# r's first six column tiles as three Strassen units, product by product, in a hybrid encoder block

## The chip, the cores and the metric

The kernel runs on one core of a Trainium2 chip. The metric is the device time of one execution in microseconds (us). A core has a matrix engine (PE, its weight loads shown as PEld), a vector engine (DVE), an activation engine (ACT), a general engine (POOL) and SyncE (SP), which here issues nearly all DMAs. Each engine takes its instructions in order, and instructions wait for each other by semaphores.

## The reference

One layer with 1024 tokens of width 1024, all in float32. What matters here:

```
h = rmsnorm(x)
q, k, v, r, lr_f, lr_b, u, g_a, g_b = split(h @ w_in)          # r has 1024 columns
o = gla(q, k, v, decay(lr_f)) + flip(gla(flip(q, k, v), decay(lr_b)))   # 4 heads, chunked, both directions
o = per_head_rmsnorm(o) * gla_norm * silu(r)
y_a = o @ w_branch_gla
y_b = pooling(u) @ w_pool_group * pool_scale
x = x + (sigmoid(g_a) * y_a + sigmoid(g_b) * y_b) @ w_out
x = x + swiglu(rmsnorm(x))                                       # w_ffn_in, w_ffn_out
out = rmsnorm(x)
```

## The kernel before

**Precision.** A float32 product is made of three fast ones: each operand is split into a high part (a cast on ACT) and a low part (the source minus the high part, on POOL or DVE, `split_to`, L200), and `products` (L271) multiplies high by high, high by low and low by high into one PSUM bank. `mm3` (L276) does that for one block of 128 x 128 weights and 512 tokens, and then calls `pump` with the work done; the text calls it a triple.

**Side work.** `pump` (L162) is the only clock: it counts triples, and after each hands out what is due. There are four lists. `put_off` (filled by `soon`) holds steps with a delay; `pending` holds splits of weights; `aside` holds generators of jobs (`beside`, L686: load, sum, cast, store, one job each time, every so many triples); `side` holds the attention of a head (`attention`, L816), a generator that yields the number of triples until its next step. So the order of instructions is fixed by counts in the program, not by time. `finish_side` and `finish_beside` run the rest of a list at once.

**Tiles.** Most data lie in 39 slots of 128 x 1024 float32 (`slot`); a load into a slot waits until the slot's last reader is done, and SP waits with it. Weights go through `wts`: four buffers `raw`, six each of `wh` and `wl`. PSUM has eight banks: three for the main products (`ps_mm`), five for the attention and other uses (`ps_g`).

**The order of the work.** The normalised features are split and stay on chip as `hT`: 16 slots, for four pairs of feature blocks, two halves of the tokens, high and low part. Then come the values and q, k of the four heads (`project_qk`, L801); beside them run the attention of the heads, the sums of the feature blocks for later (`feature_sums`, into `f_out`) and the sums of the branch weights (`branch_jobs`, into `s_out`, every 4.2 triples).

After the last k come **r's first six column tiles** (L1257 to L1291): for each tile and each half of the tokens, `feature_major` (L297) adds up eight triples in a bank. During that the attention of head 3 runs in `side`; its steps give up the ACT and DVE between them: logarithms (L843), decays (`decay`, L848, a scan on DVE), exponentials (L877 to L879), the backward sweep of states (`advance`, L910), the scores (L930), and the forward sweep (L1022), which takes the score matrix p, the stored states and the running state `sf`. The first two tiles are copied out and gated later; the others are taken through silu straight away, and `gated` (L1220) multiplies them with the head's output, stored before by heads 0 to 2 in `o_out` and loaded by `load_o`. From the fourth tile on, `feature_parts` loads the feature sums, 512 KB each, and casts and subtracts them into high and low parts for the next stage.

The **next stage** ("gates") computes r's last two tiles, u, and the two gates. It uses Strassen's scheme: two column tiles by two halves of the contraction, times two halves of the contraction by two halves of the tokens, in seven products of four triples (`Unit`, `product`, L1198) instead of eight. The operand sums of the features come from `f_out`; the weight sums are made on DVE as they are needed. Products 1, 2 and 3 use feature blocks of `hT` as they are, the others sums of them:

```
    for p, i, half in ((1, 0, 0), (2, 1, 0), (3, 1, 1)):
        right[p] = [hT.pair(2 * i + c, half) for c in range(2)]
```

Later stages (the branch projection, the output projection, the feed-forward part) use the same scheme.

Of the kernel before, what the change touches and what calls it, by code (L numbers as in the profile page):

```python
# [54 lines left out]
def kernel(  # L55
# [57 lines left out]
    def as_f32(ap):  # L113
        return ap.bitcast(F32)
# [127 lines left out]
    order += [(w_in, KT, R0 + j * P, P) for j in range(KT - 2)]  # L242
# [396 lines left out]

    right = {}  # L640
# [25 lines left out]
    def feature_parts():  # L666
        todo = [(p, c) for p in (6, 5, 7, 4) for c in range(2)]
        wholes = []

        def load_sum():  # L670
            if len(wholes) < len(todo):
                p, c = todo[len(wholes)]
                wholes.append(slot(s="hs"))
                nc.sync.dma_start(wholes[-1][:, :, :], f_out[p][:, c])

        load_sum()
        yield load_sum, None, None
        for n, (p, c) in enumerate(todo):
            yield load_sum, wholes[n][:, :, :], p
# [120 lines left out]

    def project_qk(h, last=False):  # L801
        q = slot(s="q")
        k = slot(s="k")
        for dst, scale in ((q, DK**-0.5), (k, 1.0)):
            final = last and dst is k
            w = take(not final)
            if final:
                value_weights[0].splits(2)
            elif last:
                value_weights.append(ValueWeights())  # L810
            for half in range(2):
                ps = feature_major(w, hT, half)
                nc.scalar.activation(dst[:, half, :], ps[:, :], AF.Copy, scale=scale)
        qk_heads[h] = q, k
# [252 lines left out]
    def load_o(h):  # L1067

        o_heads[h] = [slot(s="ol") for _ in range(2)]
        for half in range(2):  # L1070
            nc.sync.dma_start(o_heads[h][half][:, :, :], o_out[h][half].rearrange("(j p) t -> p j t", p=P))

# [23 lines left out]
    for h in range(HEADS):  # L1096
# [7 lines left out]
        if h == 0:  # L1104
            for ts in ((7,), (6,), (5, 4)):
                pair_products(ts)
            prepare_beside(map(branch_jobs, range(4)), 4.2)
# [110 lines left out]
    raw_r, oT, gated_o = [], {}, []  # L1218

    def gated(j, half, src, sr=None):  # L1220

        sr = t2(s="sr")[:, :] if sr is None else sr
# [4 lines left out]

        src, dst, silu = o_heads[j // 2][half], tiles[half][:, j % 2, :], sr
        if j // 2 < HEADS - 1:
            src = src[:, j % 2, :].rearrange("p (i n b) -> p n i b", i=4, b=SQ)  # L1230
            dst, silu = (t.rearrange("p (n i b) -> p n i b", n=4, b=SQ) for t in (dst, silu))
        else:
            tp = bank(ps_g, "tp")
            for i in range(4):
                nc.tensor.transpose(
                    tp[:, i * P : (i + 1) * P], src[:, i, (j % 2) * P : (j % 2 + 1) * P], ident[:, :]
                )
            src = tp[:, :]
        nc.vector.tensor_tensor(dst, src, silu, op=ALU.mult)
        there.append((j, half))  # L1240
        if len(there) == 4:
            c = j // 2 % 2
            for half, t in enumerate(tiles):
                (gated_o if j < KT - 2 else deferred).append((ob_out[j // 4, half][:, 2 * c : 2 * c + 2, :], t[:, :, :]))
            if j >= KT - 2:
                soon(2, flush)

    def put_by():

        if raw_r:  # L1250
            gated(*raw_r.pop(0))
# [5 lines left out]
    BY, PARTS_FROM = 2, 3  # L1257
    sums_begun = False
    for j in range(KT - 2):
        for h in {1: (0,), 2: (1,), 4: (2,)}.get(j, ()):  # L1260
            load_o(h)
        w = take()
        if j < BY:
            whole_r = slot(s="r")
        if j == 4:
            for _ in range(2):
                gunits[0].load()
        if j == 5:
            gates_ahead.step()
        for n, half in enumerate(reversed(range(2)) if j == KT - 3 else range(2)):  # L1270
            if j >= PARTS_FROM and not sums_begun and (j > PARTS_FROM or not side):
                finish_side()
                finish_beside()
                prepare_beside([feature_parts()], 4, quick=2)
                sums_begun = True
            ps = feature_major(w, hT, half)
            if n == 0:
                flush()
            elif j == 3:
                fetch()  # L1280
                soon(3, store_gated)
            if j < BY:
                nc.scalar.copy(whole_r[:, half, :], ps[:, :])
                raw_r.append((j, half, *[whole_r[:, half, :]] * 2))
            elif (j, half) == (BY, 0):
                soon(4, put_by, partial(gated, j, half, ps[:, :]))
            else:
                put_by()
                gated(j, half, ps[:, :])
            if j == KT - 3 and n == 0:  # L1290
                gates_ahead.step()  # L1291
    for p, i, half in ((1, 0, 0), (2, 1, 0), (3, 1, 1)):
        right[p] = [hT.pair(2 * i + c, half) for c in range(2)]


    sa_out, yb_out = (dram.tile([P, 2, KT, HALF], F32, name=n) for n in ("sa_out", "yb_out"))
# [271 lines left out]
    store_gated()  # L1568
# [613 lines left out]
```

## Time and profile before

| | |
|---|---|
| time, three runs | 1370.26, 1370.83, 1370.83 us; median 1370.83 |
| profiled execution | 1370.65 us; span from the first to the last instruction 1368.9 us |
| clock granted to PE | 0.999 |
| r's six tiles, in the span | about 263.5 to 347.5 us |

In the rows that follow, times are in us from the span's start unless marked otherwise. A row of an engine in order of time has the start, the duration, the engine, the line of the kernel, the operation, what it writes and reads, its shape and a count; in brackets stands the idle time of the engine ahead of it and what ended that. A row of waits has who waited for whom, the total in us, how often, and the longest. Names such as ps (main products), op (the attention's output), sc and p (scores), z (decays), trh and trl (high and low parts of the feature sums) are the program's. PE's matmuls are pipelined, so that the duration of one is more than the interval between two.

### The profile page before, as it was taken

To read this page: it belongs to the slowest core of one execution; us is meant where nothing else is said; L and a number is where in the kernel's file an instruction comes from. 1 tells how busy PE (TensorE), PEld (TensorE's weight loads), DVE (VectorE), ACT (ScalarE), POOL (GpSimd) and SP (SyncE) were. 2 spreads that over 40 slices of the span, in tenths; PEclk is the share of its full clock that TensorE was granted. 3 is DMA by queue.
4 is the path that set the end of the run, shared out by engine and by line. 5 is a ranking of instruction groups with operands and counts; after the bars stand their busy time and mean duration, and the time that the engine had idled before them with its cause. 6 is when DMAs were issued, how large, how long until landed. Compare 5 with 4: busy or idle time off the path is not lost. (4 is left out here: it accounts for less than half of the span.)

```text
span 1368.9 us, 17814 instructions
## 1 busy us (share of the span) xinstructions
PE 1356.6 (99%) x6262; PEld 1128.0 (82%) x6262; DVE 850.3 (62%) x1050; ACT 646.0 (47%) x1175; POOL 755.8 (55%) x561
## 2 busy tenths in 40 slices
PE   9999999999999999999999999999999999999998
PEld 7888888888788888888888888888888888888886
DVE  6975666655545767779873955565565556343375
ACT  7365665765434445554356533333333334444252
POOL 3323723223596547568764386666666667555453
PEclk9999999999999999999999999999999999999999
DMA  7321623327487669996426354555544447975552
GB/s 228 110 95 55 181 81 108 83 64 259 123 274 251 200 186 344 367 372 218 138 76 233 124 174 157 177 177 177 177 156 137 141 141 265 389 294 184 171 214 77
DMA packets 174842, 252.50 MB, mean 184 GB/s; under 512 B 11512, under 2 KB 101152, under 8 KB 174752
## 3 DMA queue, kind: packets, MB, share of 16 engines
q1 hardware_dynamic: 174608, 251.10, 54.5%
q8 instruction: 49, 0.80, 0.3%
q14 instruction: 41, 0.34, 0.1%
q10 hardware_dynamic: 144, 0.26, 0.1%
HBM read 169.27 MB, written 82.05 MB: 184 GB/s over the span
## 5 line engine op out<-in xcount | busy, mean ns | idle before, releaser
L202 POOL TENSOR_TENSOR wl<-fs,wh 128x512 fp32r<-128x512 f32 x124 | 171.8, 1390 | 162.6 <-ACT wh L201 105.1
L274 PE MATMUL ps<-gh,wh 128*128 128x512 f32 x616 | 240.5, 390 | 0.0
L274 PE MATMUL ps<-gl,wh 128*128 128x512 f32 x616 | 239.8, 389 | 0.3 <-DVE gl L1740 0.3
L274 PE MATMUL ps<-gh,wl 128*128 128x512 f32 x616 | 239.7, 389 | 0.0
L202 POOL TENSOR_TENSOR wl<-fraw,wh 128x512 fp32r<-128x512 f32 x93 | 133.0, 1430 | 71.5 <-ACT wh L201 68.9
L202 POOL TENSOR_TENSOR ol<-gor,oh 128x1024 fp32r<-128x1024 f32 (+1 forms) x42 | 101.4, 2417 | 86.0 <-ACT oh L201 71.5
L274 PE MATMUL ps<-hh,wh 128*128 128x512 f32 x356 | 144.5, 406 | 0.7 <-ACT ga L1523 0.7
L274 PE MATMUL ps<-hh,wl 128*128 128x512 f32 x356 | 138.9, 390 | 0.0
L274 PE MATMUL ps<-hl,wh 128*128 128x512 f32 x356 | 138.8, 390 | 0.0
L274 PEld LDWEIGHTS ps<-gl,wh 128*128 128x128 f32 x616 | 115.7, 188 | 24.3 <-DVE gl L1740 0.7
L274 PEld LDWEIGHTS ps<-gh,wl 128*128 128x128 f32 x616 | 115.6, 188 | 24.2
L274 PEld LDWEIGHTS ps<-gh,wh 128*128 128x128 f32 x616 | 115.7, 188 | 24.0 <-DVE sums L1906 0.2
L274 PE MATMUL ps<-oh,oh 128*128 128x512 f32 x308 | 119.8, 389 | 0.0
L274 PE MATMUL ps<-ol,oh 128*128 128x512 f32 x308 | 119.8, 389 | 0.0
L274 PE MATMUL ps<-oh,ol 128*128 128x512 f32 x308 | 119.8, 389 | 0.0
L202 POOL TENSOR_TENSOR wl<-wraw,wh 128x512 fp32r<-128x512 f32 x56 | 94.4, 1714 | 43.4 <-ACT wh L201 43.3
L202 DVE TENSOR_TENSOR ol<-wor,oh 128x1024 fp32r<-128x1024 f32 (+1 forms) x42 | 62.3, 1496 | 68.1 <-ACT oh L201 55.8
L202 POOL TENSOR_TENSOR wl<-raw,wh 128x512 fp32r<-128x512 f32 x34 | 49.7, 1472 | 85.2 <-ACT wh L201 66.2
L201 ACT CAST wh<-fs 128x512 fp32r<-128x512 f32 x124 | 76.0, 615 | 27.1 <-DVE fs L1131 26.1
L274 PEld LDWEIGHTS ps<-hh,wl 128*128 128x128 f32 x356 | 66.8, 188 | 14.2
L274 PEld LDWEIGHTS ps<-hh,wh 128*128 128x128 f32 x356 | 67.0, 188 | 13.3 <-ACT ga L1523 1.1
L274 PEld LDWEIGHTS ps<-hl,wh 128*128 128x128 f32 x356 | 67.0, 188 | 12.3
(282 smaller groups left out, 3077.4 us busy)
## 6 DMA issues: line engine op xcount, KB each, us to landing
fraw<-in_w_ffn_in_dram SPq DMA_DIRECT2D x44, 512.0 KB, 5.9
gor<-g_out SPq DMA_DIRECT2D x35, 512.0 KB, 6.6
fraw<-in_w_in_dram SPq DMA_DIRECT2D x22, 512.0 KB, 6.4
g_out<-s SPq DMA_DIRECT2D x44, 256.0 KB, 2.3
wor<-t_out SPq DMA_DIRECT2D x20, 512.0 KB, 4.7
raw<-in_w_in_dram SPq DMA_DIRECT2D x36, 256.0 KB, 4.2
g_out<-g SPq DMA_DIRECT2D x33, 256.0 KB, 2.6
x<-in_x_dram SPq DMA_DIRECT2D x16, 512.0 KB, 4.6
```

The lines of the kernel that those rows point to most:

```text
L201: nc.scalar.copy(hi, src)
L202: eng.tensor_tensor(lo, src, as_f32(hi), op=ALU.subtract)
L274: nc.tensor.matmul(ps, a[i], b[j], start=first and n == 0, stop=last and n == 2, skip_group_check=onto)
```

## The change

- r's first six column tiles become three Strassen units (`TRIO` = 3) of two tiles. They run **product by product**: product 2 of units 0, 1, 2, then product 5 of all three, and so on in the order 2, 5, 3, 1, 6, 7, 4, with 21 products of four triples in all. Each unit holds one PSUM bank; products 2 and 5 are copied out of it by ACT, 3 goes onto 5's bank and is copied, 1 starts a bank in which 6, 7 and 4 go on, with what the copies hold added by DVE.
- The weight sums for products 3, 5, 6 and 7 of each unit are made beside the attention by POOL (`r_jobs`) and stored to `r_out`; the branch sums go every 2.8 triples instead of 4.2, and `r_jobs` every 2 after them. In the r stage each product loads its 256 KB of weights (`r_load`, five products ahead) and splits them (`r_split`, three ahead); it had been 512 KB and two splits for a whole tile.
- The feature sums are loaded by an explicit list of events in the r stage (`load_sums`, `cast_sum`, `low_sum`): 5's ahead of the stage and at its first products, then 6's, 7's and 4's.
- Each row of r is gated when both its halves are there (`gate_row`); o is loaded by halves (`load_ol`).
- The feature block that product 2 uses is stored to memory after the first head's values (`store_block`) and loaded again near the end of the stage (`load_block_again`), so that its four slots are free between.

The diff, cut to its core:

```
-    order += [(w_in, KT, R0 + j * P, P) for j in range(KT - 2)]
...
+    def r_jobs(u):
+        raw = [slot(F32, (KT, P), "rraw")[:, :, :] for _ in range(2)]
+        a11, a12, a21, a22 = (t[:, 4 * j : 4 * j + 4, :] for t in raw for j in range(2))
+        yield from loading(
+            [w_in[:, c0 : c0 + P].rearrange("(k p) c -> p k c", p=P) for c0 in (R0 + 2 * u * P, R0 + (2 * u + 1) * P)], raw
+        )
+        for op, dst, a, b, p in (
+            (padd, a22, a21, a22, 5), (psub, a21, a11, a21, 7), (psub, a11, a22, a11, 6), (psub, a12, a12, a11, 3)
+        ):
+            yield partial(op, dst, a, b), None, r_out[u][p]
...
-    def feature_parts():
...
+    def load_sums(p):
+        sums_in[p] = [slot(F32R, s="trl")[:, :, :] for _ in range(2)]
+        for c, t in enumerate(sums_in[p]):
+            nc.sync.dma_start(as_f32(t), f_out[p][:, c])
+
+    def cast_sum(p, c):
+        hi, lo = slot(F32R, s="trh")[:, :, :], sums_in[p][c]
+        right.setdefault(p, []).append((hi, lo))
+        nc.scalar.copy(hi, as_f32(lo))
+
+    def low_sum(p, c):
+        hi, lo = right[p][c]
+        nc.vector.tensor_tensor(lo, as_f32(lo), as_f32(hi), op=ALU.subtract)
...
+    R_PRODUCTS = 2, 5, 3, 1, 6, 7, 4
+    r_sequence = [(u, p) for p in R_PRODUCTS for u in range(TRIO)]
...
     def project_qk(h, last=False):
...
+            begun = h == HEADS - 1 and dst is k
+            if begun:
+                finish_beside()
+                load_sums(R_PRODUCTS[1])
+                for n in range(4):
+                    r_load(n)
             for half in range(2):
                 ps = feature_major(w, hT, half)
                 nc.scalar.activation(dst[:, half, :], ps[:, :], AF.Copy, scale=scale)
+                if begun:
+                    r_split(half)
+        if begun:
+            r_load(4)
+            r_split(2)
...
+            store_block()
+            prepare_beside(map(branch_jobs, range(4)), 2.8)
+            prepare_beside(map(r_jobs, range(TRIO)), 2)
...
+    def r_evict(u, p, ps):
+        rows = r_rows[u]
+        if p in (2, 5):
+            rows[p == 5] = slot(s="r")
+        i, half = {2: (0, 0), 1: (0, 0), 3: (0, 1), 6: (0, 1), 5: (1, 1), 7: (1, 1), 4: (1, 0)}[p]
+        dst = rows[i][:, half, :]
+        if p in (2, 5, 3):
+            nc.scalar.copy(dst, ps)
+            return
+        if p != 4:
+            add(dst, ps, dst)
+            ps = dst
+        nc.scalar.activation(dst, ps, AF.Silu)
...
+    for p in R_PRODUCTS:
+        if p not in FIRST[:2] and p != 3:
+            at = TRIO * R_PRODUCTS.index(p)
+            if p != 5:
+                event(at - 5, partial(load_sums, p))
+            event(at - 3, partial(cast_sum, p, 0))
+            event(at - 2, partial(cast_sum, p, 1), partial(low_sum, p, 0))
+            event(at - 1, partial(low_sum, p, 1))
+    for u in range(TRIO):
+        event(11 + u, partial(load_ol, u, 0))
+        event(14 + u, partial(gate_row, u, 0))
+        event(15 + u, partial(load_ol, u, 1))
+        event(19 + u, partial(gate_row, u, 1))
+    event(17, partial(load_block_again, 0))
+    event(18, partial(load_block_again, 1))
+    event(16, *[gunits[0].load] * 2)
+    event(14, finish_side)
...
+    for n, (u, p) in enumerate(r_sequence):
+        if n:
+            flush()
+        r_load(n + 5)
+        r_split(n + 3)
+        for step in r_events.get(n, ()):
+            step()
+        if p in (2, 5, 1):
+            r_banks[u] = bank(ps_mm)
+        ps = r_banks[u]
+        product(lambda p, k: r_weight(u, p, k), p, ps, right)
+        r_evict(u, p, ps[:, :])
```

More of the change, by code (lines that the diff above doesn't have):

```diff
@@ L1226, in gated @@
         tiles, there = oT[j // 2]
[L1228 to L1239, printed above, removed]
+        o = o_heads[j // 2][half]
+        tp = bank(ps_g, "tp")
+        for i in range(4):
+            nc.tensor.transpose(tp[:, i * P : (i + 1) * P], o[:, i, (j % 2) * P : (j % 2 + 1) * P], ident[:, :])
+        nc.vector.tensor_tensor(tiles[half][:, j % 2, :], tp[:, :], sr, op=ALU.mult)
         there.append((j, half))
@@ L1243, in gated @@
             for half, t in enumerate(tiles):
[L1244 to L1251, printed above, removed]
+                deferred.append((ob_out[j // 4, half][:, 2 * c : 2 * c + 2, :], t[:, :, :]))
+            soon(2, flush)
     def store_gated():
@@ L1255, in store_gated @@
             nc.sync.dma_start(*gated_o.pop(0))
[L1257 to L1291, printed above, removed]
@@ L1292, with load_ol, gate_row @@
     for p, i, half in ((1, 0, 0), (2, 1, 0), (3, 1, 1)):
         right[p] = [hT.pair(2 * i + c, half) for c in range(2)]
+    r_rows = [[None, None] for _ in range(TRIO)]
+    r_banks, ol = {}, {}
+    def load_ol(u, i):
+        ol[u, i] = slot(s="ol")
+        nc.sync.dma_start(ol[u, i][:, :, :], o_out[u].rearrange("a (j p) t -> j p a t", p=P)[i])
+    def gate_row(u, i):
+        j, row = 2 * u + i, r_rows[u][i]
+        for half in range(2):
+            dst = row[:, half, :]
+            turned_product(dst, ol[u, i][:, half, :], dst)
+            gated_o.append((ob_out[j // 4, half][:, j % 4, :], dst))
+        soon(3, store_gated)
@@ L1296 @@
+    for step in r_events[len(r_sequence)]:
+        step()
     sa_out, yb_out = (dram.tile([P, 2, KT, HALF], F32, name=n) for n in ("sa_out", "yb_out"))
```

62 lines of the change are left out of this document (42 added, 20 removed).

## The prediction

> **What bounds the kernel now.** I read the totals first, then the waits of the matrix engine, its order of time in the r stage, and last the queues of ACT and DVE there. The totals (busy us, share, instructions):
>
> ```profile
> span 1368.9 us, 17814 instructions
> PE 1356.6 (99%) x6262; PEld 1128.0 (82%) x6262; DVE 850.3 (62%) x1050; ACT 646.0 (47%) x1175; POOL 755.8 (55%) x561
> ```
>
> The matrix engine (PE) is busy all the time, but busy time of pipelined matmuls does not by itself show a limit; its waits do. In the chain of waits, PE rows only (us in total, times, longest):
>
> ```profile
> PE ps L274 <- ACT ga L1523: 1.3, 2, 0.7
> PE ps L274 <- POOL wl L202: 0.6, 2, 0.4
> PE op L274 <- DVE p L202: 0.4, 2, 0.2
> PE op L274 <- ACT p L201: 0.3, 1, 0.3
> ```
>
> The rows make 2.6 us in 1369. So PE's own stream is the bound, and a matmul taken out is worth its issue interval, unless something else then comes late. The interval, from the first and the last of 69 matmuls of the r stage with nothing between them (start us, us):
>
> ```profile
> 263.54 0.39 PE L274 MATMUL ps<-hh,wh 128*128 128x512 f32 x1
> ...
> 278.95 0.40 PE L274 MATMUL ps<-hh,wl 128*128 128x512 f32 x1
> ```
>
> (278.95 - 263.54) / 68 = 0.227 us; three of them, one row block in split precision ("a triple"), 0.68 us. The r stage in three windows (length, then busy us and count of PE, PEld, DVE, ACT, POOL; clock, DMA share, GB/s):
>
> ```profile
> 263.50:300.00 36.50, 36.50 (x186) 30.85 (x186) 22.72 (x38) 26.42 (x52) 14.58 (x14) 1.00 0.41 120
> 300.00:320.50 20.50, 20.50 (x124) 18.26 (x123) 11.73 (x27) 12.24 (x37) 3.55 (x3) 1.00 0.40 129
> 320.50:347.50 27.00, 27.00 (x121) 22.36 (x120) 18.82 (x22) 13.76 (x21) 8.41 (x5) 1.00 0.70 234
> ```
>
> PE never waits in these 84 us. The first two windows also carry the attention of head 3, whose steps run between the triples; there ACT is busy 72% and 60%. That is the cover to watch.
>
> **The change part by part.** *Matmuls.* Six column tiles are 6 x 2 halves x 8 blocks x 3 = 288 matmuls; three units of seven products are 3 x 7 x 4 x 3 = 252. The transposes of head 3's output are as many as before. 36 x 0.227 = **-8.2 us**. [...]
>
> *Weight sums beside the attention.* Twelve POOL operations, six loads of 512 KB, twelve stores of 256 KB, in the steps that the branch sums leave when they go every 2.8 triples and not every 4.2: 31 steps x 4.2 = 130 triples before, 31 x 2.8 + 24 x 2 = 135 after (four times seven steps, three times seven, and three to drain each), and 144 triples lie between their start and the last k projection, where `finish_beside` would run what is left. One operation, and one split:
>
> ```profile
> L715 POOL TENSOR_TENSOR wsum<-wsum x16: 1270/1291/1742, 115.1 to 423.1; 128x512 f32<-128x512 f32 x16
> L202 POOL TENSOR_TENSOR wl<-raw,wh x34: 1271/1294/2549, 34.9 to 329.4; 128x512 fp32r<-128x512 f32 x34
> ```
>
> 12 x 1.29 = 15.5 us more on POOL over some 150 us; behind one of them a split or a q product comes at most 1.3 us late. Bounds: -0.6 (the POOL waits of PE vanish) to +2.6 (two such hits); I take 0. The feature block's four stores and four loads of 512 KB lie on SP; PE used these tiles long before the store and needs the reload only in the next stage.
>
> *The r stage's other work.* Splits go from 12 to 21, evictions on ACT from 16 operations (4 copies, 12 silus) to 21 (9 and 12), DVE gets 9 additions. The eight casts and eight residuals of the feature sums stay eight, but come earlier: before, the first cast was at 321.4, after head 3's attention; now product 5's two stand at the stage's first products, and those of 6 and 7 in the attention's forward sweep. ACT, in order of time, with the idle time ahead in brackets, and the rows of the sums (min/median/max ns):
>
> ```profile
> 264.36 0.64 ACT L813 ACTIVATE k<-ps 128x512 f32<-128x512 f32 x1
> 265.01 1.28 ACT L843 ACT_TABLE_LOAD   x1
> 266.31 2.05 ACT L843 ACTIVATE z<-z 128x512 f32<-128x512 f32 x4
> ...
> 273.74 0.62 ACT L201 CAST wh<-raw 128x512 fp32r<-128x512 f32 x1
> 274.26 0.60 ACT L877 ACTIVATE qe<-z 128x512 f32<-128x512 f32 x1
> ...
> 278.70 0.59 ACT L1283 COPY r<-ps 128x512 f32<-128x512 f32 x1 [2.72 <-PE ps L274]
> ...
> 285.75 0.20 ACT L879 ACTIVATE fac<-tot 128x8 f32<-128x8 f32 x1
> ...
> 297.00 0.59 ACT L201 CAST p<-sc 128x512 fp32r<-128x512 f32 x1
> ...
> 311.40 0.51 ACT L923 ACTIVATE sf<-st,fac 128x256 f32<-128x256 f32 x1 [0.16 <-DVE st L919]
> ...
> 312.61 0.60 ACT L201 CAST wh<-raw 128x512 fp32r<-128x512 f32 x1
> ```
> ```profile
> L709 ACT CAST trh<-hs x8: 1047/1055/1063, 321.4 to 342.4; 128x1024 fp32r<-128x1024 f32 x8
> L700 DVE TENSOR_TENSOR trl<-hs,trh x8: 1212/1218/2322, 324.7 to 347.6; 128x1024 fp32r<-128x1024 f32 x8
> ```
>
> Back to back a 512-column ACT operation takes 0.52 (273.74 to 274.26). DVE's decay, and the scores' residual:
>
> ```profile
> 266.92 0.69 DVE L850 TENSOR_TENSOR la<-la,z 128x512 f32<-128x512 f32 x1 [2.11 <-ACT z L843]
> 267.78 1.23 DVE L862 TENSOR_TENSOR_SCAN z<-la,carry 128x511 f32<-128x511 f32 x1
> 269.24 0.43 DVE L868 TENSOR_TENSOR z<-z,tot 128x256 f32<-128x256 f32 x1
> ...
> 270.43 2.21 DVE L862 TENSOR_TENSOR_SCAN z<-la,carry 128x511 f32<-128x511 f32 x1
> ...
> 297.62 0.69 DVE L202 TENSOR_TENSOR p<-sc,p 128x512 fp32r<-128x512 f32 x1 [0.65 <-ACT p L201]
> ```
>
> First place, product 5 (fourth product, needs its second residual 14 triples into the stage: 263.54 + 14 x 0.68 + 0.23 = 273.3). ACT's queue from 264.36: k's eviction 0.52, three casts 1.56, first sum cast 1.05, table 1.28, logarithms 2.05, an eviction and a cast 1.04, second sum cast 1.05: 272.9. DVE adds 1.22: 274.1. PE waits **0.8**. Bounds: 0 (ACT reaches the first casts earlier) to 1.9 (the residual at its longest, 2.32).
>
> Second place, the score matrix p. The logarithms start at 268.8, not 266.3. From 274.1 DVE does three more decays of 2.75 (266.92 to 269.67) to 3.8 (scan 2.3) and four products or residuals of 0.6: 284.8 to 287.9, with short waits for ACT some 287.2; the fourth exponentials (1.2) end at 288.4, against 285.95 (285.75 + 0.20): 2.4 late. Until p ACT then does three evictions, three casts and a sum cast, 4.2 us, where it had a copy and two casts, 1.6; 0.5 of the rest goes into its idle time. So p's cast moves from 297.0 to 297.0 + 2.4 + 2.1 = 301.5, and p is whole 1.3 later, 302.8. PE's use of it, and of the first forward state sf:
>
> ```profile
> 299.95 0.28 PE L274 MATMUL op<-vh,p 128*128 128x256 f32 x1
> ...
> 303.36 0.59 PE L1035 MATMUL op<-sf,qe 128*128 128x256 f32 x2
> ...
> 311.74 0.27 PE L274 MATMUL op<-vh,p 128*128 128x256 f32 x1
> ...
> 314.00 0.28 PE L274 MATMUL op<-vh,p 128*128 128x256 f32 x1
> ```
>
> 299.95 + 0.8 = 300.75, so PE waits **2.0**. Bounds: 0 (all decays at 2.75, and all bursts in idle time) to 4 (every scan at 2.3 and nothing hidden).
>
> Third place, sf. Between p and the first forward state ACT gets a table load, two silus, two casts and a sum cast (4.4), and DVE two additions and two residuals ahead of it, the second behind that sum cast; sf comes 4.8 after p, PE uses it 3.4 after (303.36 - 299.95): **1.4**, bounds 0 to 2.5. The sweep's later bursts fit: a step is 2.3 us of PE (311.74 to 314.00) and 1.2 of ACT (311.40 to 312.61).
>
> *After the attention* ACT and DVE have room (third window: 51% and 70%). Queued by SP from product 13 up to the block's second half: 1792 + 768 + 1280 + 2048 + 1536 + 1024 KB = 8.65 MB (sums of 4, weights, o, stores of the gated rows, the next unit's weights, the block). The rate that the queues keep up where they are full:
>
> ```profile
> 547.00:582.00 35.00, 35.00 (x155) 28.84 (x154) 25.14 (x25) 18.47 (x31) 21.08 (x14) 1.00 0.98 368
> ```
>
> 8.65 MB / 368 = 23.5 us; PE needs the block's second half 38 triples and two forward steps later, 26 + 2 = 28 us. Cost 0 (bounds 0, and the rival below). The two waits of the next stage (1.3, ACT ga) I leave as they are, bounds -1.3 to +1.3.
>
> Sum: -8.2 + 0.8 + 2.0 + 1.4 = -4.0. The profiled execution took 1370.65 (span 1368.9), 0.2 under the median 1370.83; from the median **1366.8**.
>
> **The rivals.** *All of it is kept.* If ACT's idle time (2.72 in the quoted row alone) takes the added casts, no place costs over 0.3: 1362.6 to 1363. For it: PE waits nowhere in the stage now. Against: the sum of ACT's queue up to product 5 has no idle time left in it.
>
> *The chain eats all of it.* Where POOL works beside it, DVE is slow: the scan at 267.78 took 1.23, most of it before these two splits, and the one at 270.43 took 2.21:
>
> ```profile
> 269.00 2.55 POOL L202 TENSOR_TENSOR wl<-raw,wh 128x512 fp32r<-128x512 f32 x2 [9.24 <-ACT wh L201]
> ```
>
> The residuals took 1.22 at best and 2.32 at worst. If nine more splits hit two scans and four residuals, that is 2 x 1 + 4 x 1.1 = 6.4 more on DVE, of which some 4 reach PE: 1370.8, no change. [...]
>
> *Slower: the reload comes late.* If the queues move what stands from product 13 on at the 234 GB/s of the third window and not at 368, 8.65 MB take 37.0 us, 9 over the 28: 1366.8 + 9 = 1375.8. It turns the gain into a loss from 4.0 us of wait on, that is below 8.65 MB / 32 us = 270 GB/s. For it: weight blocks come in short rows from the input matrix, and SP stands still behind a load that waits for a slot. Against: that window's share is 0.70, so 234 is demand and not the limit.
>
> **How the numbers follow.** The forecast (1364 to 1368.5) gets 0.44, all kept 0.19, eaten 0.25, slower 0.12. 0.2% is 2.7 us, about what a measurement of this kernel tells from no change: faster (under 1368.1) 0.44 + 0.19 less 0.02 that lies above the line, same 0.27, slower 0.12. The range from 1362.6 to 1371.5 leaves out most of the slow case and the edges. The forecast's own range is 1364 to 1368.5.
>
> **What the profile after would show.** Right: 6226 matmuls; in PE's waits, rows of a few tenths to 2 us at ps behind a trl residual near 273, at op behind p near 300, at op behind sf near 305; ACT over 85% busy from 264 to 305. All kept: no such rows and a stage of 75.8 us. Eaten: the same rows, longer, and scans and residuals all over 2 us. Slower: a wait of ps for a DMA at the first product 2 after the r stage. The prediction is wrong if PE waits for wl of the r products, which I cost at nothing (three products, 8 us, ahead), or if slots hold SP back so that these weights come late.

## The result, and the profile after

| | before | after |
|---|---|---|
| median of the runs on one chip | 1370.83 us (4 runs) | 1387.38 us (1386.65 to 1387.83, 4 runs) |
| ratio, 95% interval | | 1.0121 [1.0103, 1.0138] |
| profiled execution; its span | 1370.65; 1368.9 us | 1387.01; 1385.3 us |

The change made the kernel 1.2% slower; the forecast was 0.3% faster. The totals of the page after (span, then busy us, share and number of instructions of each engine):

```profile
span 1385.3 us, 17868 instructions
PE 1355.8 (98%) x6226; PEld 1123.8 (81%) x6226; DVE 855.8 (62%) x1059; ACT 653.0 (47%) x1189; POOL 781.0 (56%) x582
```

The 36 matmuls are gone (6262 to 6226), and yet the span is 16.4 us longer. In the chain of waits, the rows of the matrix engine PE (us in total, times, longest):

```profile
PE ps L273 <- POOL wl L202: 7.5, 4, 6.1
PE op L273 <- ACT p L201: 5.1, 2, 4.9
PE ps L273 <- DVE trl L693: 2.7, 3, 1.3
PE ps L273 <- ACT ga L1603: 1.7, 2, 1.1
PE ps L273 <- ACT wh L201: 1.1, 1, 1.1
PE ps L273 <- DMA hl<-h_out: 1.1, 2, 0.8
```

Before, the four such rows made 2.6 us; now these six make 19.2. PE in order of time shows the two large ones, with the last matmul ahead of each:

```profile
220.76 0.39 PE L273 MATMUL ps<-hl,wh 128*128 128x512 f32 x1
227.21 0.79 PE L273 MATMUL ps<-hh,wl 128*128 128x512 f32 x1 [6.06 <-POOL wl L202]
...
311.04 0.39 PE L273 MATMUL ps<-hh,wl 128*128 128x512 f32 x1
316.32 0.58 PE L273 MATMUL op<-vh,p 128*128 128x256 f32 x1 [4.89 <-ACT p L201]
```

The first lies 42 us ahead of the r stage, in the projection of head 3's q; the second in the r stage, at the score matrix. Behind both the clock is granted by half, as the windows show (busy us and count of PE, PEld, DVE, ACT, POOL; then the clock, DMA share, GB/s):

```profile
224.00:227.00 3.00, 0.00 (x0) 0.00 (x0) 0.76 (x2) 0.45 (x2) 3.00 (x4) 0.50 1.06 315
227.00:230.00 3.00, 2.79 (x8) 2.41 (x9) 0.04 (x1) 0.00 (x0) 3.00 (x5) 0.50 0.56 154
230.00:233.00 3.00, 3.00 (x17) 2.55 (x17) 1.52 (x3) 1.85 (x5) 2.92 (x3) 0.93 0.23 87
...
316.00:318.00 2.00, 1.68 (x6) 1.46 (x7) 1.70 (x3) 0.65 (x2) 0.23 (x1) 0.50 0.36 78
...
320.00:322.00 2.00, 2.00 (x7) 1.71 (x7) 0.69 (x1) 0.97 (x4) 0.17 (x1) 0.50 0.26 58
```

Where the time went, by three places that both traces have: the first of head 3's z matmuls, the first r product, and the first copy of a gate. Before, and after:

```profile
257.16 0.40 PE L825 MATMUL z<-lrT,up 128*128 128x512 f32 x1
262.18 0.39 PE L274 MATMUL ps<-hh,wh 128*128 128x512 f32 x1
352.80 0.58 ACT L1523 COPY ga<-ps 128x512 f32<-128x512 f32 x1
```
```profile
264.57 0.40 PE L887 MATMUL z<-lrT,up 128*128 128x512 f32 x1
269.59 0.39 PE L273 MATMUL ps<-hh,wh 128*128 128x512 f32 x1
369.25 0.58 ACT L1603 COPY ga<-ps 128x512 f32<-128x512 f32 x1
```

The z matmul starts 7.4 us later than before: the wait of 6.06 us and some 1.6 us of work lost to the half clock behind it, less what other places gave. From the first r product to the first copy of a gate it is 99.7 us where it was 90.6; with 8.2 us of matmuls less, that is 17.2 us lost. The waits in this stretch make 10.8 of them, the half clock from 316.3 to 322.6 some 3.1. Of the other 3.3 about 0.16 lie at each of the nine waits, 1.5 in all: a wait is counted from the end of the last matmul's row (311.04 + 0.39 + 4.89 = 316.32), and the next matmul could have started 0.23 behind that row's start, the interval in the r stage before (0.227). The remaining 1.8 us are not placed. Behind the first gate both kernels run alike: 7.4 + 9.0 = 16.4.

What made the first wait is in the queues. SP (which issues the transfers), its row in the waits of that stretch, and POOL, in order of time:

```profile
195.68 11.15 SPq L563 DMA_DIRECT2D o_out<-ot  x8
...
209.52 1.94 SPq L597 DMA_DIRECT2D rraw<-in_w_in_dram  x2
```
```profile
SPq L563 <- DVE ot L1071: 7.4, 1, 7.4
```
```profile
217.00 1.30 POOL L742 TENSOR_TENSOR rraw<-rraw 128x512 f32<-128x512 f32 x1 [14.57 <-DMA rraw<-in_w_in_dram]
...
225.89 1.26 POOL L202 TENSOR_TENSOR wl<-raw,wh 128x512 fp32r<-128x512 f32 x1
```

SP is held for 11 us by head 1's eight output stores. It does not issue all that time: the first four go out from 195.68 to 197.54, the last four from 205.00 to 206.84, and between them SP stands 7.4 us for a tile that DVE still has to transpose (`ot`). The next unit's two weight blocks, behind them in SP's queue, are asked for only at 209.5. POOL's next instruction is the sum of these blocks, and it stands still for 14.6 us in front of it. Behind that sum in its queue are head 2's q products and the low part of head 3's weights, which PE needs at 221.0 and gets at 227.2.

What made the second, on ACT and on DVE:

```profile
280.82 1.47 DVE L693 TENSOR_TENSOR trl<-trl,trh 128x1024 fp32r<-128x1024 f32 x1 [3.65 <-ACT trh L689]
282.22 0.68 DVE L912 TENSOR_TENSOR la<-la,z 128x512 f32<-128x512 f32 x1
```
```profile
285.12 0.62 ACT L201 CAST wh<-rr 128x512 fp32r<-128x512 f32 x1 [2.84 <-DMA rr<-r_out]
...
312.40 1.28 ACT L1335 ACT_TABLE_LOAD   x1
313.70 0.63 ACT L1335 ACTIVATE r<-r 128x512 f32<-128x512 f32 x1
314.23 0.60 ACT L201 CAST wh<-rr 128x512 fp32r<-128x512 f32 x1
314.74 1.04 ACT L689 CAST trh<-trl 128x1024 fp32r<-128x1024 f32 x1
315.69 0.58 ACT L201 CAST p<-sc 128x512 fp32r<-128x512 f32 x1
```

The first decay of head 3 (`la`) stands on DVE behind product 5's second low, its exponentials on ACT behind a split whose load is late (2.84 us), and at the end p's cast behind a silu with its table load, a split and the cast of product 6's sum. Which of these weighs what is a matter for the experiments.

### The profile page after: what moved, and what is told of

Its sections match the earlier page's. It is cut to its first block, busy times and chain, and to the rows that moved or that the text cites. A ratio compares the mean times of both kernels' runs of the same rounds, so it can differ in the third digit from the quotient of the medians.

```text
span 1385.3 us, 17868 instructions
## 1 busy us (share of the span) xinstructions
PE 1355.8 (98%) x6226; PEld 1123.8 (81%) x6226; DVE 855.8 (62%) x1059; ACT 653.0 (47%) x1189; POOL 781.0 (56%) x582
## 5 line engine op out<-in xcount | busy, mean ns | idle before, releaser
L273 PE MATMUL ps<-hh,wl 128*128 128x512 f32 x296 | 116.6, 394 | 6.7 <-POOL wl L202 6.7
L273 PE MATMUL ps<-hh,wh 128*128 128x512 f32 x296 | 120.8, 408 | 1.7 <-ACT wh L201 1.1
L273 PE MATMUL ps<-hl,wh 128*128 128x512 f32 x296 | 116.3, 393 | 1.1 <-DMA hl<-h_out 1.1
L273 PE MATMUL ps<-trl,wh 128*128 128x512 f32 x224 | 87.6, 391 | 2.7 <-DVE trl L693 2.7
L273 PE MATMUL ps<-trh,wh 128*128 128x512 f32 x224 | 88.9, 397 | 1.1 <-ACT ga L1603 1.1
L273 PE MATMUL ps<-trh,wl 128*128 128x512 f32 x224 | 87.3, 390 | 0.0
L273 PEld LDWEIGHTS ps<-hh,wl 128*128 128x128 f32 x296 | 56.1, 189 | 19.5 <-POOL wl L202 7.6
```

Of the source, the lines that this page charges most:

```text
L273: nc.tensor.matmul(ps, a[i], b[j], start=first and n == 0, stop=last and n == 2, skip_group_check=onto)
```

## The experiments

### Round 1: the two large waits

Two kernels take the first wait apart. One leaves out the weight sums (products 3, 5, 6 and 7 read plain blocks of the input weights instead); the other does all of the work, but asks for a unit's blocks before the sums of the unit ahead of it:

```
e1_no_weight_sums
-            prepare_beside(map(r_jobs, range(TRIO)), 2)
e2_loads_ahead
     def r_jobs(u):
+        if u == 0:
+            yield partial(r_loads, 0), None, None
+        if u + 1 < TRIO:
+            yield partial(r_loads, u + 1), None, None
...
```

> Leaves out the weight sums beside the attention (the r stage loads plain blocks of the input matrix in place of the sums of products 3, 5, 6 and 7); the products, splits and casts stay. Theory A, two late pieces: PE's 6.06 us wait for a weight's low part at 227 in the changed kernel comes from POOL standing at a weight sum whose load is late; it goes, and with it the stretch at half clock behind it, so the time falls by 7.4 us (the lag of head 3's first z matmul against the kernel before) to 1380.0. Rival B, the r stage alone is too dense: the wait at 227 costs only its 6.06 less what waits later anyway, and the time falls by less than 4 us, to over 1383.

> All of the work as in the changed kernel, but the loads of the next unit's blocks for the weight sums are issued ahead of the sums of the unit before (two slots more). Theory A: POOL finds its data, the wait at 227 and the half clock behind it go, 1380.0 as without the sums. Rival C, the twelve POOL sums and 6 MB of transfers are too much beside the attention whenever they are issued: the wait stays within 2 us of 6, and the time at 1385 or more.

Measured: 1378.9 us (1.0057 [1.0042, 1.0072]) and 1379.2 us (1.0061 [1.0045, 1.0076]). In both the wait of 6.06 us and the half clock behind it are gone, and the wait for p (4.9) is as before. So the first place costs some 8 us (8.2 by the medians; 7.4 by the z matmuls above, and in e2's profile the half clock behind p was also shorter, 3.4 us and not 6.8). It is the late load alone: in e2 SP still goes through the same stores from 196.94 to 208.09, with the next unit's loads ahead of them at 185.9, and no row of POOL from 195 to 228 us has a wait for one of these loads. The sums themselves, their transfers and the time of POOL cost nothing that can be told from the spread of these runs (1377.9 to 1380.5 us in e1, 1377.9 to 1381.9 in e2), since doing them all with an earlier load is as fast as leaving them out.

Two more kernels leave out product 5's and 6's feature sums (plain feature blocks in their place: four loads, four casts and four lows fewer), one of them the weight sums as well:

```
e3_no_feature_casts
-                load_sums(R_PRODUCTS[1])
...
-        if p not in FIRST[:2] and p != 3:
+        if p in (7, 4):
...
+    for p, i, half in (..., (5, 0, 0), (6, 1, 1)):
         right[p] = [hT.pair(2 * i + c, half) for c in range(2)]
e4_neither: both edits
```

> Leaves out the feature sums of products 5 and 6 (plain feature blocks stand in for them): four loads, four casts on ACT and four residuals on DVE fewer in and ahead of the r stage. Theory A: the 4.89 us wait for the score matrix p comes from ACT and DVE reaching it late because these casts and residuals stand ahead of it; at least 3.5 of it go, with the 6 us at half clock behind it (3 us lost), so the time falls by 6.5 to 9 us, to 1378.5 to 1381. Rival D, ACT is late because SP stands at the output stores of head 2 and the splits wait for their weights (2.84 us at 285): p stays 3 us or more late, 1384 or more.

> Both left out together: no weight sums beside the attention and no feature sums of 5 and 6. Theory A, the two add up: 1387.4 - 7.4 - 7.7 = 1372, within 2. If they share a cause (the second is late only because the first shifted the queues), the sum is smaller: 1376 or more. If nothing else were late it would be 1362.6, the time before less 36 matmuls.

Measured: 1383.0 us (1.0086 [1.0069, 1.0102]) and 1376.25 us (1.0039 [1.0025, 1.0052]). The casts and lows of the sums are only half of the second place: without them p still comes 2.66 and 2.41 us late, and e3 lies between its two theories. e4 lies at the edge of "1376 or more", but not by a shared cause: e3's edit gave 4.4 us and not 7.7, and 8.4 (e1) and 4.4 added up make 1374.5, within the spread of e4's runs (1374.97 to 1379.25). Why p stays late, e4 shows; DVE and ACT at the start of head 3's chain:

```profile
268.87 0.69 DVE L911 TENSOR_TENSOR la<-la,z 128x512 f32<-128x512 f32 x1 [3.64 <-ACT z L904]
```
```profile
276.94 0.62 ACT L201 CAST wh<-rr 128x512 fp32r<-128x512 f32 x1 [2.10 <-DMA rr<-in_w_in_dram]
...
278.88 0.60 ACT L938 ACTIVATE qe<-z 128x512 f32<-128x512 f32 x1
```

The decay now starts at once behind its logarithm and is done by 271.6, but its exponential comes at 278.9, behind a split that waits for its load. Counted from ACT's copy of k (266.37 in e2, 264.77 in e4), the decay starts 5.8 us earlier than in e2 (276.24), and the exponential (279.31 in e2) no earlier, even 1.2 us later. Two delays lay side by side, each alone long enough to hide the other.

### Round 2: the start of the chain

Three kernels on top of e2 take these two away, one each and both; a fourth moves the rest of the stage's side work as well.

```
g_five_before
                 if begun:
                     r_split(half)
+                    if half == 0:
+                        for c in range(2):
+                            cast_sum(5, c)
+                            low_sum(5, c)
g_stores_behind
-        flush()                      (attention, ahead of Ln)
+        if h < HEADS - 1:
+            flush()
...
-        if n:                        (r loop)
+        if n > 4:
             flush()
g_both: both edits
h_all, on top of g_both: block 1's split with block 0's; for products 6, 7, 4
+            event(at - 6, partial(load_sums, p))
+            event(at - 4, partial(cast_sum, p, 0))
+            event(at - 3, partial(cast_sum, p, 1), partial(low_sum, p, 0))
+            event(at - 2, partial(low_sum, p, 1))
     and load_block_again at 15 and 16 instead of 17 and 18
```

> All of the work, loads one unit ahead as in e2 (1379.2 us), and product 5's two feature casts and lows issued while head 3's k is projected, ahead of the r stage. Theory P (two waits lie side by side ahead of head 3's exponentials: the low of product 5 ahead of the first decay on VectorE, and the split of weight block 6, whose load stands behind head 2's eight o_out stores on SyncE, ahead of the first exponential on ScalarE; each alone is long enough): the first decay starts some 7 us earlier, the exponentials at most 1 us earlier, the wait for p stays 3 to 5 us, 1376 to 1379 us. Theory D (the low on VectorE alone delays p): the wait for p of 4.9 us goes and the half clock behind it with it, 1371.5 us.

> As e2, and head 2's eight o_out stores queued behind the r stage's first loads instead of ahead of weight block 6's load. Theory P: the first decay still waits for the low of product 5 (at 276.2 us in e2), so the exponentials start at most 0.5 us earlier and p still waits 4 to 5 us: 1378 to 1379.5 us. Theory S (the stores alone delay p): 1371.5 us.

> Both edits of g_five_before and g_stores_behind, on top of e2. Theory P: head 3's exponentials start 4 to 6 us earlier, p is there when TensorE wants it (wait under 0.5 us), the half clock behind the wait goes: 1379.2 - 4.9 - 3 = 1371.3 us, within 1.5. Theory Q (p's cast waits on ScalarE's own queue, for the first silu with its table load, the split and the cast of a sum that stand ahead of it, however early the chain is): 2.4 us or more of the wait stay, 1375 to 1377 us.

> g_both, and every other work of the stage one step earlier: weight block 1's split with block 0's, the sums of products 6, 7 and 4 cast and split one product earlier, feature block 0 loaded again two products earlier. Theory P, with each wait of TensorE worth its length: r's start 1.7, the lows of products 7 and 4 2.2, the load of block 0 1.0 less than g_both: 1366.5 us, within 2. The theory that these short waits are hidden or only move on: as g_both within 1 us.

Measured, against e2's 1379.2: 1380.9, 1378.4, 1382.1 and 1384.9 us (ratios 1.0074 [1.0059, 1.0089], 1.0054 [1.0038, 1.0071], 1.0077 [1.0062, 1.0092], 1.0097 [1.0081, 1.0114]; one of g_stores_behind's four executions took 7618 us and is left out, with it the median is 1379.4). Only the second came out as its theory said (p still 4.4 us late). In the first p's wait is as theory P had it (3.6 us), but the time is above its range; the third and fourth refute what I expected of them. The reason is a place that I had not looked at. DVE and PE in g_both:

```profile
259.44 2.61 DVE L702 TENSOR_TENSOR trl<-trl,trh 128x1024 fp32r<-128x1024 f32 x2 [1.97 <-ACT trh L698]
261.97 0.41 DVE L1112 COPY o<-op 128x256 f32<-128x256 f32 x1
```
```profile
270.37 0.50 PE L273 MATMUL ps<-hh,wh 128*128 128x512 f32 x1 [4.08 <-ACT wh L201]
```

The two lows went ahead of the last copy of head 2's output, behind that copy head 3's first gate on ACT came at 264.65 instead of 261.84, and the splits of the next r weights, queued behind the gates, made PE wait 4.1 us where it had waited 1.1 (4.1 in g_five_before too). In h_all the waits for lows 7 and 4 and for block 0 were gone, but the load of the first gate weights, now behind block 0's on SP, landed so late that ACT stood 6.4 us in front of its cast, with r's silus queued behind it, and PE waited 3.4 us for the bank.

### Round 3: the same, into idle time

ACT stood idle from 259.1 to 261.8 us in e2. j_chain puts product 5's casts and the splits of blocks 1 and 2 there, and the lows behind the projection; j_chain_soon takes the first silus away from in front of p's cast; j_all moves products 7 and 4 and the reload one product forward.

```
j_chain, on top of g_stores_behind
+                if begun and half == 0:
+                    r_split(0)
+                    soon(0.7, partial(cast_sum, 5, 0), partial(cast_sum, 5, 1), partial(r_split, 1), partial(r_split, 2))
+                elif begun:
+                    for c in range(2):
+                        low_sum(5, c)
j_chain_soon, on top of it
+        if p == 1:
+            soon(2, partial(nc.scalar.activation, dst, ps, AF.Silu))
j_all, on top of it: for products 7 and 4 the events at - 6, - 4, - 3, - 2;
     load_block_again at 16 and 17, behind the gate unit's loads
```

> All of the work. Loads one unit ahead and head 2's stores behind, as in g_stores_behind (1379.4 us); while the second half of head 3's k is projected, in the time in which ScalarE stood idle in e2 (259.1 to 261.8 us), product 5's two casts and the splits of weight blocks 1 and 2; product 5's lows behind that projection, so that VectorE's last copies of head 2 go ahead of them (in g_both the lows went first and head 3's gates came 2.7 us later). Theory P' (what p lacks is the late start of head 3's Ln and first decay, behind the splits and casts on ScalarE and the low on VectorE): no wait for wh at r's start (1.1 in e2), none for product 5's low, Ln some 2 us and the first decay some 6 us earlier than in e2 against r's start, the wait for p under 1 us and no half clock behind it: 1379.4 - 1.7 - 0.6 - 4.4 - 2.5 = 1370 us, within 2. Theory Q (p's cast is late by what stands ahead of it on ScalarE's own queue in product 10: silu with its table load, a split, a cast of a sum): 2.4 us or more of the wait for p stay, 1374 us or more.

> j_chain, and the silus of product 1 issued some 2 us later, so that p's cast can go ahead of the first one and of its table load. Theory P': as j_chain, within 1 us, since p is in time there. Theory Q: the wait for p is 2 us shorter than in j_chain.

> j_chain_soon, and the casts and lows of products 7 and 4 one product earlier, feature block 0 loaded again one product earlier, with the first gate unit's weight loads still ahead of it. Theory P': the waits for the lows of products 7 and 4 (0.9 and 1.3 us in e2) and for block 0 (0.95 us) go: 2 to 3 us less than j_chain_soon, 1367 to 1368 us. The theory that these waits only move on: within 1 us of j_chain_soon.

Measured: 1374.3 us (1.0027 [1.0017, 1.0037]), 1372.4 us (1.0011 [1.0001, 1.0020]) and 1373.0 us (1.0014 [1.0005, 1.0023]). The waits for wh and for product 5's low are gone, as expected. p is still 3.11 us late in j_chain, and 1.64 in j_chain_soon, 1.5 less where theory Q had 2: so the queue ahead of p's cast is a cause by itself (theory Q). ACT in j_chain:

```profile
300.84 1.28 ACT L1348 ACT_TABLE_LOAD   x1
302.13 0.63 ACT L1348 ACTIVATE r<-r 128x512 f32<-128x512 f32 x1
302.67 0.60 ACT L201 CAST wh<-rr 128x512 fp32r<-128x512 f32 x1
303.18 1.04 ACT L698 CAST trh<-trl 128x1024 fp32r<-128x1024 f32 x1
304.12 0.57 ACT L201 CAST p<-sc 128x512 fp32r<-128x512 f32 x1
```

From the table load to p's cast there is no idle time. j_all gained nothing: the waits for the two lows went (2.2 us), and a wait of 1.0 us for a sum of r and one of 1.8 us for block 0 came in their place; its loads were asked for earlier, but SP then stood 3.2 us at the first of them (336.81 to 340.05); no row shows what for.

### Round 4: the waits that were left

```
k_six, on top of j_chain_soon: for products 7 and 4 the events one product earlier, for product 6
+            event(n, partial(soon, 2, step))
k_gate, on top of it
-        event(14 + u, partial(gate_row, u, 0))
+        event(16 + u, partial(gate_row, u, 0))
m_two, on top of k_six: r's first copy on nc.vector, soon(6, ...) for product 1's silus
m_three, on top of m_two
+        event((14, 16, 17)[u], partial(gate_row, u, 0))
n_silu, on top of m_three: product 1's silus as event(11 + u, ...)
n_silu_act: n_silu with r's first copy on nc.scalar
```

> j_chain_soon (1372.4 us), and product 6's casts and lows issued some 2 us later than in it, so that the casts of head 3's keys and of p on ScalarE and the score matrix's copy on VectorE go ahead of them; products 7 and 4's casts and lows one product earlier (as in j_all), block 0's reload left where the change has it. Theory Q' (what is left of the wait for p is the queue: one cast of 1.0 us ahead of the keys and one low of 1.2 us ahead of the score matrix): the wait for p goes from 1.6 to under 0.3 us. With the lows of 7 and 4 (2.2 us) less 1.0 us for the bank that waits for a sum of r instead, as in j_all: 1372.4 - 1.5 - 1.2 = 1369.7 us, within 1. Theory P (what is left is the chain itself, begun too late): the wait for p stays at 1.3 us or more, 1371 us or more.

> k_six, and the first three gate rows of r two products later, so that VectorE takes the lows of product 4 and r's sums first. If the 1.0 us that product 4 waits for r's sum is the gate row ahead of it: 1 us less than k_six, 1368.7 us, slightly faster than before. If the rows' slots come free too late for the loads of the gates' weights and of block 0, which wait for them on SyncE: a longer wait at the gates' start, 1370 us or more.

> k_six (1370.9 us), with the first eviction of r on VectorE (in k_six product 5 waits 0.8 us for its bank, whose copy stands behind Ln on ScalarE) and the silus of product 1 issued 6 instead of 2 us later (in k_six TensorE waits 1.1 us for sf, behind the casts and silus on ScalarE). Theory W (every wait of TensorE in this stage is on the path and worth its length, so the gain of 8.2 us appears as far as the waits go): 0.8 + 1.1 = 1.9 us less than k_six, 1369 us. Theory M (the waits only move on: what fills the stage is the sum of the work beside it): within 0.7 us of k_six.

> m_two, and the second and third gate row of r one product later, behind the sums of r that product 4 waits for (1.1 us in k_six). Theory W: 1 us less than m_two, 1368 us, if the slots for block 0's reload do not come free later; if they do, the wait for block 0 grows by as much, and it is as m_two. Theory M: as k_six.

> m_three (1371.9 us), with the silus of product 1 issued two products later by a step of their own: in m_three they stood at the head of the list of put-off steps, and product 6's low behind them in that list came 1.9 us too late. Theory W (each wait is worth its length): 1371.9 - 1.9 = 1370.0 us, and 1 us less if the wait for sf (0.6) goes as well, 1369 to 1370 us. Theory M (the waits only move): 1371.5 us or more.

> n_silu, with r's first eviction on ScalarE again. If that copy is worth its wait (0.8 us in k_six against 0.24 in m_three): 0.5 us slower than n_silu. If it holds up head 3's first decay on VectorE as much as it saves: the same within 0.3 us.

| | median us | ratio, 95% interval |
|---|---|---|
| k_six | 1370.9 | 1.0002 [0.9993, 1.0011] |
| k_gate | 1373.2 | 1.0015 [1.0006, 1.0024] |
| m_two | 1373.0 | 1.0014 [1.0005, 1.0023] |
| m_three | 1371.9 | 1.0010 [1.0002, 1.0019] |
| n_silu | 1371.6 | 1.0002 [0.9993, 1.0011] |
| n_silu_act | 1370.8 | 0.9999 [0.9990, 1.0008] |

k_six nearly settles p: with product 6's casts and lows out of the way its wait is 0.51 us (theory Q' had under 0.3, theory P 1.3 or more). It is as fast as the kernel before, 16.5 us faster than the change, and still 8 us slower than the saving would make it. PE's rows with a wait in its r stage and behind it:

```profile
271.88 0.50 PE L273 MATMUL ps<-trh,wh 128*128 128x512 f32 x1 [0.81 <-ACT r L1343]
302.29 0.39 PE L273 MATMUL op<-vh,p 128*128 128x256 f32 x1 [0.51 <-ACT p L201]
307.57 0.70 PE L1110 MATMUL op<-sf,qe 128*128 128x256 f32 x2 [1.12 <-ACT sf L998]
339.57 0.47 PE L273 MATMUL ps<-trh,wh 128*128 128x512 f32 x1 [1.07 <-DVE r L1346]
349.35 0.50 PE L273 MATMUL ps<-hl,wh 128*128 128x512 f32 x1 [0.70 <-DMA hl<-h_out]
351.88 0.50 PE L273 MATMUL ps<-hl,wh 128*128 128x512 f32 x1 [0.75 <-DMA hl<-h_out]
```

From the first r product (262.75) to the first gate's copy (353.06) k_six takes 90.3 us; before it was 90.6. The 8.2 us are saved and lost again: 5.4 us in waits, most of them of half a microsecond to one, some 1.3 in the 0.16 us at each of eight, and about 1 that is not placed.

Taking more of them away did not help. In k_gate the wait for r's sum went, and block 0 came later, by the second branch of its expectation:

```profile
351.26 0.79 PE L273 MATMUL ps<-hh,wh 128*128 128x512 f32 x1 [3.10 <-DMA hh<-h_out]
```

In m_two the list of put-off steps held product 6's low behind a silu (1.91 us, the edit's own fault), and its time lies above both of its theories; m_three has the same wait and lies 1.0 us above k_six. In n_silu that was mended, and r's copy and r's sum cost almost nothing any more (0.2 us), but sf came late twice (0.93 and 0.62) and waits for block 0's loads cost 0.5, 1.0 and 1.8. n_silu_act fits neither branch of its expectation: it is 0.8 us faster than n_silu, which is less than the spread of either.

The list of waits changed from kernel to kernel, but in the profiles of all six the waits of the stage add up to 5.4 to 6.8 us (k_six and n_silu_act least, m_two most), and the medians stayed at 1371 to 1373: the waits moved on, as theory M has it. Theory W, that a wait is worth its length, is not refuted by these medians, because the clock differed too. It was at half for 3.4 us in n_silu's profile and for 6.8 in those of k_gate, m_two and n_silu_act, each time at block 0's waits (in m_two 3.4 us of it earlier, behind product 6's low), and never in those of k_six and m_three. The executions of n_silu_act whose mean granted clock was 0.999 or 1.000 took 1369.4 to 1370.8 us, those of the kernel before beside it 1370.3 to 1371.6: where the clock holds, some 1 us of the saving may be left. That no order of this work could do better is not shown, and no kernel tried here beats the one before by its median.

## Why the prediction was wrong

The mechanism of the gain was right: 36 matmuls went, and PE's stream was the bound. Of the three places named in the r stage two showed at once (product 5's low and p), the third (sf) only when p was in time. The other places, and most of the sizes, were missed.

*Weight sums beside the attention, costed at 0 (bounds -0.6 to +2.6): measured 8.2 (after against e2; 7.4 by the lag at head 3's z).* This was the largest miss, and it is one of kind: I counted instructions on POOL and did not follow the DMA that each needs on SP. A sum whose load stands behind stores that hold SP for 11 us (7.4 of them for a tile that is not there yet) stops POOL's whole queue; the bound should have been the time that POOL stands for the load, 14.6 us here, and not one or two hits of 1.3 us. I had followed SP's queue only for the feature block and the end of the stage.

*Second place, p, 2.0 us (bounds 0 to 4): measured 4.9 of wait and some 3 us of half clock behind it.* The step that failed is the order of the queues. I let the stage begin at 263.54, where a run of matmuls without anything between them begins; the first product of r starts two triples earlier, at 262.18. So I counted due steps from the wrong start: product 5's second low goes ahead of the first decay and not behind it, and the first silu with its table load, a split and a cast go ahead of p's cast. The wait in three parts, by experiment: the chain's start 1.8 us (4.91 in e2 to 3.11 in j_chain, of which the stores behind gave 0.6), the silu 1.5 (to 1.64, j_chain_soon), product 6's cast and low 1.1 (to 0.51, k_six). One reading in that term was wrong the other way: it let PE wait for p's residual, 1.3 us behind the start of its cast, but PE's first matmul there started at 316.32, when the cast alone was done (315.69 + 0.58); by that the term would have been 1.3 and not 2.0.

*First place, product 5's low, 0.8 us: measured 0.55.* *Third place, sf, 1.4: nothing while p was late; 1.1 us in k_six, where p was in time.* Both are inside their bounds. ACT was to be over 85% busy up to p; it was busy 78% of 270 to 312 us (32.63 of 42), because it stood for late loads and for DVE as well.

*The splits of r's own weights, costed at nothing: 1.07 for wh and 0.62 for wl at the stage's start.* The prediction named this as what would make it wrong; the second to fourth split stand on ACT behind head 3's gates, so "three products ahead" was true in the program and not in time.

*Products 7 and 4, not costed: 0.88 and 1.32 for their lows.* *Reload of block 0, 0: 0.27 and 0.80.* The rival that put a loss of 9 us there named the wrong place; the loss came, by others. That DVE's scans would grow and eat the gain was not it either: head 3's four scans took 7.3 us after (1.47, 2.24, 1.64, 1.90) and 7.0 before (1.23, 2.21, 2.30, 1.23), and the time lay in queue order.

*The half clock* was in no term. With it the wait of 4.9 cost some 8 us, and that of 6.1 some 7.7.

Of the 16.5 us by which the change is slower, then, e2 gives back 8.2, and the steps from there over j_chain and j_chain_soon to k_six together 8.3, most of it at p. The forecast of 1366.8 was reached by none of them.

## What to carry to other kernels

An instruction that is added to an in-order queue costs what stands behind it waits for (here a sum behind a late load held POOL for 14.57 us, and PE for 6.06), so each added step has to be followed to its own transfer, and that transfer to what stands ahead of it on the queue that issues it. A delay that has two causes side by side can show nothing when one is taken away (in e4 the decay came 5.8 us earlier and the exponential 1.2 later): read the chain's start in the experiment's own trace before dropping a theory. Where PE is the bound at 99%, a saving of 0.6% of its work (8.2 us) is no larger than what the waits of a new schedule can cost (5.4 us of waits in the best ones here, 16.8 in the change, the clock not counted), and the work that runs beside it has to be ordered before the saving is counted.

## What the hardware did that I had not expected

A wait of PE cost more than its length when the clock fell to half with it (in the change 6.06 us cost some 7.7, and 4.89 some 8), and this is not a matter of the length alone. The granted clock was at half for 6.83 us with each of the waits of 6.06 and 4.89 in the change, and for 6.8 with the 2.41 of e4; for 3.4 with the 4.91 of e2 and the 3.11 of j_chain; with the 2.66 of e3 not at all. Even the two short waits at the start of r, 1.06 and 0.63 us with two matmuls between them, were followed by some 3.4 us of half clock in e1, e3 and e4 (in e1 PE's matmuls start 0.43 us apart from 268.14 to 271.12, and 0.23 apart from 271.45 on), and by none in the change and in e2. m_two and m_three do the same work in the same order up to this wait, and their profiles differ. PE's row in m_two and in m_three:

```profile
313.93 0.50 PE L273 MATMUL ps<-trl,wh 128*128 128x512 f32 x1 [1.91 <-DVE trl L702]
```
```profile
313.91 0.50 PE L273 MATMUL ps<-trl,wh 128*128 128x512 f32 x1 [1.91 <-DVE trl L702]
```

And the windows behind it (the clock is the third number from the end), in m_two and in m_three:

```profile
314.00:316.00 2.00, 2.00 (x10) 1.79 (x11) 0.60 (x2) 1.30 (x4) 0.00 (x0) 0.79 0.00 0
316.00:318.00 2.00, 2.00 (x7) 1.62 (x6) 0.91 (x2) 1.14 (x4) 0.00 (x0) 0.50 0.57 154
```
```profile
314.00:316.00 2.00, 2.00 (x13) 1.83 (x13) 0.69 (x3) 1.30 (x4) 0.00 (x0) 1.00 0.00 0
316.00:318.00 2.00, 2.00 (x14) 1.79 (x13) 0.88 (x3) 1.30 (x4) 0.01 (x1) 1.00 0.66 170
```

The same wait of 1.91 us is followed by half clock in one execution (3.4 us of it) and by full clock in the other. The stretches have a pattern: each stretch of half clock that was read between 200 and 380 us was some 3.41 us long or twice that (223.59 to 230.42 and 315.76 to 322.59 in the change, 6.83 each), and where one execution has several, their starts lie whole multiples of this length apart: 92.17 us in the change (27 times 3.414), 40.96 in e1 (267.92 and 308.88; 12 times 3.413), 37.55 in e4 (268.34 and 305.89; 11 times 3.414), 37.54 in m_two (315.18 and 352.72; 11 times 3.413). So it may be where a wait falls in such a beat that decides; that is an estimate from these four distances, and no run tests it. Gaps of 1.9 us, and of 1.06 and 0.63 together, were followed by half clock; how long a gap has to be is not shown.

The clock also goes with the spread of the times. m_three's four executions with a mean granted clock of 0.999 or 1.000 took 1370.28 to 1370.96 us, its four with 0.995 or 0.996 took 1373.24 to 1375.17; the kernel before, beside it at 0.999, took 1370.5 to 1372.0. That is a match over executions; nothing here sets the clock by itself.
